# Sparse attention on one core: a new start, scores by halves, half masks near the end, and moved transposes

## Chip, cores, metric

The kernel runs on one core of one Trainium2 chip. The metric is the device time of the whole kernel in microseconds (us), as the median of several executions. A profile's span is about 1.8 us shorter than the time of the same execution (233.0 us against 234.81 us in the kernel before). Engines in the profile: PE is the matmul engine, PEld its weight loads, DVE the vector engine, ACT the scalar engine, POOL the GpSimd engine, SP the engine that issues the loads.

## The reference

Attention over 4 x 8 = 32 heads, 512 queries, 1024 keys, head size 64, with a random mask in which about 10% of the entries are 1. All inputs are fp32. The mask alone is 64 MiB of the 88.08 MB that are read.

```python
def reference(q, k, v, sparse_mask):
    scale = 1.0 / np.sqrt(q.shape[-1])
    scores = scale * np.matmul(q, k.transpose(0, 1, 3, 2))
    scores = np.where(sparse_mask > 0, scores, -1e9)
    attn = np.exp(scores - np.max(scores, axis=-1, keepdims=True))
    attn = attn / (np.sum(attn, axis=-1, keepdims=True) + 1e-8)
    return np.matmul(attn, v).astype(np.float32)
```

## The kernel before

Scores are made with keys on the partitions. A matmul of a mask block against 30 times the identity adds 30 to the entries that stay, and the exp takes 30 away again, so the mask costs matmuls and nothing else. A head has four steps (g = 0 to 3). In each, PE makes scores and adds the mask, ACT takes the exp of 128x1024 elements, and PE multiplies with v one step later.

```python
def scores(h, g):                      # heads 0 to 29
    stg = p_st.tile([128, 2, SQ], FP32, name="stg")
    for i in range(2):                 # two key tiles, all 512 queries
        c = 2 * g + i
        nc.tensor.matmul(stg[:, i, :], kt(h, c), qt(h, c, 0, NQ), start=True, stop=False)
    for i in range(2):
        for t in range(NQ):            # needs all four query blocks of the mask
            nc.tensor.matmul(stg[:, i, ts(t, 128)], mask_weights(h, t, 2 * g + i), cid[:],
                             start=False, stop=(t == NQ - 1))
    pt = expo(stg, [128, 2, SQ])
    return lambda: values(h, g, pt)
# ... heads 30 and 31 go by quarters of the queries, with their masks loaded in quarters ...

with tc.manual_schedule(engines=ordered):      # every engine runs in program order
    for n in range(3):
        load(n)                                # n = 0: mask, then q, k, then v
    # ... constants ...
    convert_qk(0)
    for step in range(4):
        transposes(0, step)                    # q and k of four heads, turned by PE, copied by DVE
    convert_v(0)
    steps = {(1, 2): 0, (2, 0): 1, (2, 2): 2, (3, 1): 3}
    pending = lambda: None
    for h in range(NHEADS):
        if h + 3 < NHEADS:
            load(h + 3)                        # every fourth also loads q, k of the next four heads
        for g in range(NG):
            if g == 1 and h + 1 < NHEADS:
                convert_v(h + 1)
            if (h % GH, g) == (1, 1) and following:
                convert_qk(following)
            todo = quarter_scores(h, g) if quarters else scores(h, g)
            if (h % GH, g) in steps and following:
                transposes(following, steps[h % GH, g])
            pending()
            pending = todo
```

The softmax here doesn't subtract the row's maximum and nothing guards it: scores larger than these inputs give would overflow.

## Time and profile before

| | |
|---|---|
| time | 234.78 us median of 4 (234.44 to 235.03) |
| span of the profile | 233.0 us |
| PE busy | 190.3 us (82%) |
| DMA engines | busy from the second of 40 slices to the 38th |
| mean rate | 398 GB/s over the span, 400 to 436 GB/s in nearly all full slices |

These are lines of the page of the kernel before: span, busy time of PE, the busy tenths of PE, PE's granted clock, busy tenths and rate of the DMA engines in 40 slices, the DMA queue of kind "instruction", and the shares of the chain that ended last.

```profile
span 233.0 us, 5967 instructions
...
PE 190.3 (82%) x2608; PEld 144.1 (62%) x2608; DVE 129.7 (56%) x228; ACT 143.8 (62%) x129; POOL 18.3 (8%) x39
...
PE   0022589899989998999899859996799959999993
...
PEclk9999999999999999999999988999799997999999
DMA  7999999999999999999999999999999999999931
GB/s 239 416 432 425 425 419 422 415 429 425 425 422 400 436 414 427 419 417 435 407 431 417 420 431 418 424 405 436 423 421 419 410 429 427 416 421 403 368 115 23
...
q8 instruction: 20, 0.33, 0.6%
...
DMA 41%; PE 30%; DVE 16%; ACT 8%; issue 3%; SPq 1%; ACTq 0%
...
```

DMA is at 9 (90% or more) nearly throughout, PE is not: the input stream sets the pace.

The next lines are from the timeline of the start of the kernel before (start, duration, engine, line, operation, and in brackets the idle time before and its releaser).

```profile
...
9.85 1.29 DVE L101 TENSOR_SCALAR q<-qf 128x1024 f16<-128x1024 f32 x2 [9.85 <-DMA qf<-in_q_dram]
...
13.50 2.41 DVE L127 COPY qT<-tp 128x512 f16<-128x512 f16 x2
...
15.97 1.04 PE L123 MATMUL tp<-id,q 128*128 128x128 f16 x8 [3.74 <-DVE qT L127]
...
26.61 0.61 PE L157 MATMUL stg<-qT,kT 64*128 64x512 f16 x2 [2.52 <-DVE kT L127]
...
```

PE's first transposes have to wait for a vector copy of 2.4 us before the next ones can use the one PSUM buffer, and the first scores come at 26.61 us.

The timeline of the kernel before around the end of head 25 and the start of head 26:

```profile
...
188.01 0.71 PE L162 MATMUL stg<-cid,mask 128*128 128x128 bf16 x8
...
189.63 0.43 DVE L134 CAST v<-vf 128x512 f16<-128x512 f32 x1 [2.41 <-DMA vf<-in_v_dram]
...
191.32 0.62 PE L123 MATMUL tp<-id,q 128*128 128x128 f16 x8 [2.60 <-DVE q L101]
...
193.80 0.61 PE L157 MATMUL stg<-qT,kT 64*128 64x512 f16 x2
...
194.85 1.07 PE L162 MATMUL stg<-cid,mask 128*128 128x128 bf16 x8 [0.44 <-DMA mask<-in_sparse_mask_dram]
...
```

PE stops at 188.7 us, in the middle of head 25, because the transposes wait for a conversion of q (2.60 us of idle), which the vector engine does only after a conversion of v that itself waits for a load. Then the scores of one step of head 25 (192.12 us) and the values of its last steps are still to do. The first mask matmul of head 26 is at 194.85 us, released by the mask load. Its eight matmuls take 1.07 us, where the usual figure is 0.72.

The timeline of the kernel before at the first mask weights of head 29:

```profile
...
213.04 0.60 PEld L162 LDWEIGHTS <-mask 128*128 128x128 bf16 x8 [0.41 <-DMA mask<-in_sparse_mask_dram]
...
```

The load released them after 0.41 us. The timeline of the kernel before at the end, from the mask matmuls of the last quarter:

```profile
...
227.66 0.72 PE L213 MATMUL stg<-cid,mask 128*128 128x128 bf16 x8
...
229.64 0.43 PE L227 MATMUL av<-v,pt 128*128 128x65 f16 x8 [0.81 <-ACT pt L150]
...
230.32 0.28 DVE L237 TENSOR_SCALAR o<-av,rz 128x64 f32<-128x64 f32 x1
```

Head 29 is the last whose mask PE waited for. From there PE runs without a wait of more than 0.3 us, except for the last exp (0.81 us).

### The profile page before, as it was taken

To read this page: it belongs to the slowest core of one execution; us is meant where nothing else is said; L and a number is where in the kernel's file an instruction comes from. 1 tells how busy PE (TensorE), PEld (TensorE's weight loads), DVE (VectorE), ACT (ScalarE), POOL (GpSimd) and SP (SyncE) were. 2 spreads that over 40 slices of the span, in tenths; PEclk is the share of its full clock that TensorE was granted. 3 is DMA by queue.
4 is the path that set the end of the run, shared out by engine and by line. 5 is a ranking of instruction groups with operands and counts; after the bars stand their busy time and mean duration, and the time that the engine had idled before them with its cause. 6 is when DMAs were issued, how large, how long until landed. Compare 5 with 4: busy or idle time off the path is not lost.

```text
span 233.0 us, 5967 instructions
## 1 busy us (share of the span) xinstructions
PE 190.3 (82%) x2608; PEld 144.1 (62%) x2608; DVE 129.7 (56%) x228; ACT 143.8 (62%) x129; POOL 18.3 (8%) x39
## 2 busy tenths in 40 slices
PE   0022589899989998999899859996799959999993
PEld 0011367677777677777677637774677747766782
DVE  0267506883688358845884177822796156851232
ACT  0000167768866886788677816687277854778873
POOL 2000001010101010101010000100000000101000
PEclk9999999999999999999999988999799997999999
DMA  7999999999999999999999999999999999999931
GB/s 239 416 432 425 425 419 422 415 429 425 425 422 400 436 414 427 419 417 435 407 431 417 420 431 418 424 405 436 423 421 419 410 429 427 416 421 403 368 115 23
DMA packets 14890, 92.66 MB, mean 398 GB/s; under 512 B 2768, under 2 KB 2768, under 8 KB 9872
## 3 DMA queue, kind: packets, MB, share of 16 engines
q1 hardware_dynamic: 13424, 88.35, 91.5%
q0 software_dynamic: 1440, 3.93, 4.3%
q8 instruction: 20, 0.33, 0.6%
q14 instruction: 6, 0.05, 0.1%
HBM read 88.08 MB, written 4.19 MB: 396 GB/s over the span
## 4 chain that ended last, share of the span: by engine, by line
DMA 41%; PE 30%; DVE 16%; ACT 8%; issue 3%; SPq 1%; ACTq 0%
DMA mask<-in_sparse_mask_dram 36%; PE stg L162 10%; DVE qT L127 9%; ACT pt L150 7%; PE av L179 6%; PE stg L157 5%; DMA kf<-in_k_dram 4%; PE tp L123 4%; DVE k L107 2%; PE stg L213 2%; DVE kT L127 2%; DVE q L101 1%; PE stg L204 1%; PE av L227 1%; DVE oo L193 1%
## 5 line engine op out<-in xcount | busy, mean ns | idle before, releaser
L150 ACT ACTIVATE pt<-stg,biasC 128x1024 f16<-128x1024 f32 x128 | 142.5, 1114 | 57.5 <-PE stg L162 50.6
L162 PEld LDWEIGHTS <-mask 128*128 128x128 bf16 x960 | 72.8, 152 | 30.7 <-issue 26.6
L162 PE MATMUL stg<-cid,mask 128*128 128x128 bf16 x960 | 90.0, 240 | 1.5 <-DMA mask<-in_sparse_mask_dram 1.4
L179 PE MATMUL av<-v,pt 128*128 128x65 f16 x960 | 50.8, 197 | 2.8 <-ACT pt L150 1.0
L157 PE MATMUL stg<-qT,kT 64*128 64x512 f16 x240 | 48.5, 400 | 2.5 <-DVE kT L127 2.5
L179 PEld LDWEIGHTS <-pt 128*128 128x128 f16 x960 | 40.0, 100 | 8.0 <-ACT pt L150 8.0
L127 DVE COPY qT<-tp 128x512 f16<-128x512 f16 x32 | 39.8, 1344 | 9.1 <-PE tp L123 9.1
L127 DVE COPY kT<-tp 128x512 f16<-128x512 f16 x32 | 39.9, 1346 | 5.1 <-PE tp L123 5.1
L191 DVE RECIPROCAL rz<-av 128x4 f32<-128x4 f32 x30 | 5.6, 186 | 59.2 <-PE av L179 59.2
L199 POOL DMA_DIRECT2D out_dram<-oo x30 | 17.1, 570 | 201.9 <-DVE oo L193 201.9
L123 PE MATMUL tp<-id,q 128*128 128x128 f16 x128 | 11.1, 236 | 25.9 <-DVE q L101 20.1
L123 PEld LDWEIGHTS <-q 128*128 128x128 f16 x128 | 8.5, 107 | 27.2 <-DVE q L101 20.7
L150 ACT ACT_TABLE_LOAD x1 | 1.3, 1283 | 28.3 <-PE stg L162 28.3
L134 DVE CAST v<-vf 128x512 f16<-128x512 f32 x32 | 13.4, 421 | 8.8 <-DMA vf<-in_v_dram 8.8
L157 PEld LDWEIGHTS <-kT 64*128 64x128 f16 x240 | 11.5, 93 | 9.5 <-DVE kT L127 2.8
L101 DVE TENSOR_SCALAR q<-qf 128x1024 f16<-128x1024 f32 x16 | 10.3, 685 | 9.8 <-DMA qf<-in_q_dram 9.8
L123 PE MATMUL tp<-id,k 128*128 128x128 f16 x128 | 10.7, 231 | 6.1 <-DVE kT L127 2.5
L193 DVE TENSOR_TENSOR oo<-av,rz 128x256 f32<-128x256 f32 x30 | 12.7, 424 | 1.2
L123 PEld LDWEIGHTS <-k 128*128 128x128 f16 x128 | 8.2, 103 | 7.6 <-DVE kT L127 2.8
L107 DVE CAST k<-kf 128x2048 f16<-128x2048 f32 x8 | 9.7, 1215 | 1.2 <-DMA kf<-in_k_dram 1.2
L213 PE MATMUL stg<-cid,mask 128*128 128x128 bf16 x64 | 5.7, 233 | 0.0
L213 PEld LDWEIGHTS <-mask 128*128 128x128 bf16 x64 | 4.7, 150 | 0.8
(16 smaller groups left out, 18.1 us busy)
## 6 DMA issues: line engine op xcount, KB each, us to landing
mask<-in_sparse_mask_dram SPq DMA_DIRECT2D x29, 2048.0 KB, 27.1
kf<-in_k_dram SPq DMA_DIRECT2D x8, 1024.0 KB, 27.2
vf<-in_v_dram SPq DMA_DIRECT2D x16, 512.0 KB, 25.9
qf<-in_q_dram SPq DMA_DIRECT2D x8, 512.0 KB, 26.3
mask<-in_sparse_mask_dram SPq DMA_DIRECT2D x8, 512.0 KB, 20.2
out_dram<-oo POOLq DMA_DIRECT2D x30, 128.0 KB, 6.5
mask<-in_sparse_mask_dram SPq DMA_DIRECT2D x2, 1024.0 KB, 6.3
out_dram<-o SPq DMA_DIRECT2D x8, 32.0 KB, 1.8
```

The lines of the kernel that those rows point to most:

```text
L101: nc.vector.tensor_scalar_mul(out=q16[:, :, x, :], in0=g["qf"][:].rearrange("p (r d) -> p r d", r=RQ), scalar1=scale,)
L107: nc.vector.tensor_copy(out=k16[:].rearrange("p r d -> p (r d)"), in_=g["kf"][:])
L123: nc.tensor.transpose(tp[:, a, e, :], src, ident16[:])
L127: nc.vector.tensor_copy(out=dst[:, :, :, j::GH].rearrange("m x e p -> m e x p"), in_=tp[:, a, :, :].rearrange("m e (x p) -> m e x p", x=GH),)
L134: nc.vector.tensor_copy(out=v16[:, :, 0:D], in_=S[h]["vf"].rearrange("p (t d) -> p t d", t=NK))
L150: nc.scalar.activation(out=pt[:], in_=stg[:], func=EXP, bias=biasC[:], scale=1.0)
L157: nc.tensor.matmul(stg[:, i, :], kt(h, c), qt(h, c, 0, NQ), start=True, stop=False)
L162: nc.tensor.matmul(stg[:, i, ts(t, 128)], mask_weights(h, t, 2 * g + i), cid[:], start=False, stop=(t == NQ - 1),)
L179: nc.tensor.matmul(st["av"][:, t, :], pt[:, i, ts(t, 128)], st["v16"][:, c, :], start=(c == 0 and t == 0), stop=(c == NK - 1), skip_group_ ...
L193: nc.vector.tensor_tensor(out=oo[:], in0=av[:, :, 0:D], in1=rz[:].broadcast_to([128, NQ, D]), op=MULT,)
L199: nc.gpsimd.dma_start(os_[:, h, :], oo[:].rearrange("p t d -> p (t d)"))
L213: nc.tensor.matmul(stg[:, c % 2, c // 2, :], mask_weights(h, t, c), cid[:], start=False, stop=True, skip_group_check=True,)
```

## The change

The intent: q and k first and two engines for the first copies, so that PE starts earlier; scores by half of the queries and half of the keys, so that a head can begin with half its mask; masks 26 to 29 in halves for that; transposes and the conversion of v one step later; and a last exp in two pieces.

```diff
+    STEPS = [(1, 3), (2, 1), (2, 3), (3, 1)]
@@ transposes(i, step)
-        tp = p_tp.tile([128, 2, 4, 128], FP16, name="tp")
+        if i == 0 and step % 2 == 1:
+            tp = p_st.tile([128, 2, 4, 128], FP16, name="stg")
+        else:
+            tp = p_tp.tile([128, 2, 4, 128], FP16, name="tp")
 ...
-            nc.vector.tensor_copy(
+            copy = nc.scalar.copy if i == 0 and step % 2 == 1 else nc.vector.tensor_copy
+            copy(
@@ scores and values: half of the queries (y), half of the keys (g)
-    def scores(h, g):
-        stg = p_st.tile([128, 2, SQ], FP32, name="stg")
-        for i in range(2):
-            c = 2 * g + i
+    def scores(h, y, g):
+        stg = p_st.tile([128, 2, 2, 256], FP32, name="stg")
+        for i in range(4):
+            c = 4 * g + i
             nc.tensor.matmul(
-                stg[:, i, :], kt(h, c), qt(h, c, 0, NQ), start=True, stop=False
-            )
-        for i in range(2):
-            for t in range(NQ):
+                stg[:, i % 2, i // 2, :],
+                kt(h, c),
+                qt(h, c, 2 * y, 2),
+                start=(i < 2),
+                stop=False,
+                skip_group_check=True,
+            )
+        for i in range(4):
+            for t in range(2):
                 nc.tensor.matmul(
-                    stg[:, i, ts(t, 128)],
-                    mask_weights(h, t, 2 * g + i),
+                    stg[:, i % 2, i // 2, ts(t, 128)],
+                    mask_weights(h, 2 * y + t, 4 * g + i),
                     cid[:],
 ...  (values: the same loops; the first and last matmul of a group are marked to match)
@@ quarter_scores(h, t): only the last quarter of the last head
+        if h == NHEADS - 1 and t == NQ - 1:
+            sides = [
+                p_st.tile([128, NG, 128], FP32, name="stg"),
+                p_tp.tile([128, NG, 128], FP32, name="tp"),
+            ]
 ...
+        for x in range(2):
+            for c in range(x, NK, 2):
+                nc.tensor.matmul(sides[x][:, c // 2, :], mask_weights(h, t, c), cid[:], ...)
+            if h == NHEADS - 1 and t == NQ - 1:
+                exp(pt[:, x, :, :], sides[x][:])
 ...  (head 30: the four quarters are stored by one DMA instead of four)
@@ load(n)
         if n == 0:
-            load_mask(0, parts=2)
             load_qk(0)
-            load_v(0)
-            return
         if n % GH == 2 and n // GH + 1 < NHEADS // GH:
             load_qk(n // GH + 1)
-        if n % 2 == 0:
+        if n % 2 == 0 and n:
             load_v(n // 2)
-        load_mask(n, parts=mask_parts(n))
+        load_mask(n, parts=NQ if n >= NHEADS - 2 else (1 if 0 < n < 26 else 2))
+        if n == 0:
+            load_v(0)
@@ the main loop
-        steps = {(1, 2): 0, (2, 0): 1, (2, 2): 2, (3, 1): 3}
 ...
-                if g == 1 and h + 1 < NHEADS:
+                if g == 2 and h + 1 < NHEADS:
                     convert_v(h + 1)
-                if (h % GH, g) == (1, 1) and following:
-                    convert_qk(following)
-                todo = quarter_scores(h, g) if quarters else scores(h, g)
-                if (h % GH, g) in steps and following:
-                    transposes(following, steps[h % GH, g])
+                if g == 1 and x == 1 and more:
+                    convert_qk(i)
+                todo = quarter_scores(h, g) if quarters else scores(h, g // 2, g % 2)
+                if (x, g) in STEPS and more:
+                    transposes(i, STEPS.index((x, g)))
```

## The prediction

> **What bounds the kernel now.** The input stream. The page's slices show the DMA engines at 9 from the second slice to the 38th, nearly all of them at 400 to 436 GB/s; 92.66 MB at 422 GB/s are 220 us of the 233.0 us span. (The Trainium skill, "DMA: Bandwidth & Descriptors", section "Bandwidth", measured 425 GB/s for 16 MB; this trace agrees.) PE is 82% busy and starts late: the timeline shows q converted at 9.85 us, transposes and copies in turn (2.4 us of DVE copies per 1.03 us of transposes), first scores at 26.6 us. But PE has caught up by 133 us: the timeline shows it idle around 135, 163 and 190 us, released by loads of q, k, v, then by masks. The chain of waits has three mask loads of 27 to 29 us, the last ending at 213.0 us.
>
> From there PE is the limit. Head 29's mask lands whole at 213.0 us (PE waited 0.4 us). The last three heads take 5.35 us each (steps of 1.22 to 1.44 us), so the last mask matmuls end at 228.4. The trace's completion records put the last quarter of mask 31 near 225.5 us, so PE is some 2.2 us behind the stream. Then come exp 1.17, values 0.43, DVE 0.5 and the last store, to 233.0.
>
> **What the change does.**
> 1. q and k ahead of mask 0, half the first copies on ACT with a second PSUM buffer: first scores near 15 us (estimate: q lands 4 us earlier, two copy pairs of 2.4 us leave DVE). Worth almost nothing at the end: the bytes are the same and the stream was full; PE just waits more afterwards.
> 2. Scores by half of the queries and half of the keys: same columns, 240 more matmuls and weight loads. The quarter heads, with still smaller pieces, already run at 1.23 and 1.45 us a step, so no cost. The 128x1024 exp stays at 1.11 us.
> 3. Masks 26 to 29 land in halves, and PE can start on the first: 1 MB at 420 GB/s is 2.5 us earlier at head 26. Transposes after (1,3) no longer hold back scores behind q, k, v. Against it: PE idles before head 26, and after such gaps eight mask matmuls take 1.07 instead of 0.72 us (half clock, as in the Trainium skill, "TensorE: Matmul & The Clock Gate", Part 1; the windows' granted clock of 0.91 to 0.96 there agrees). Replayed with before's landing times, head 29 begins 1.8 us earlier.
> 4. The last quarter's exp in halves: 0.5 us less tail.
> 5. Head 30 stored in one DMA: off the critical path.
>
> **Sum.** 1.8 + 0.5 = 2.3 us off the critical path. Both limits then meet: PE's last step and the last mask quarter near 225.5 us, after which some 5 us are needed. Predicted: 232.4 us, 8 in 10 between 230.4 and 234.2. Chances: faster by over 2% (under 230.1) 0.11, within 2% 0.88, slower 0.01.
>
> **What would show it.** First scores near 15 us; DMA slices still full; more PE idle time before masks in the first half; a wait for the mask at the last quarters; mean step still 1.33 us; last input landing within 1 us of 225.5; two last exps of about 0.65 us.
>
> **What would make it wrong.** The last landing moving: its completions spread over 6 us, so a better balance of the DMA engines could give 2 to 3 us more, and more instruction fetches take 1. A colder PE in the last heads would eat the gain.

## The result, and the profile after

The changed kernel took 232.63 us (median of 11, 232.25 to 233.56), the kernel before 234.79 us in the same rounds. The ratio is 0.9915, with a 95% interval of 0.9900 to 0.9929. It is faster by 0.9%, within the 2% band, and 0.2 us from the predicted 232.4.

The same lines of the page, of the changed kernel:

```profile
span 230.5 us, 6446 instructions
...
PE 192.6 (84%) x2848; PEld 150.0 (65%) x2848; DVE 124.9 (54%) x224; ACT 148.8 (65%) x134; POOL 21.3 (9%) x40
...
PE   0559689996999839999499977999499996999994
...
PEclk9999958999999976999979997999979999999999
DMA  7999999999999999999999999999999999999961
GB/s 263 413 430 429 423 417 431 410 426 429 418 426 400 419 435 421 424 409 432 420 428 409 421 431 419 429 412 425 416 429 424 400 418 417 420 414 409 411 252 26
...
q8 instruction: 22, 0.36, 0.6%
...
DMA 83%; PE 10%; DVE 2%; ACT 2%; issue 1%; ACTq 0%; SPq 0%
...
```

The stream is as full as before; the chain is now 83% DMA. Queue 8 has 22 pieces instead of 20.

The timeline of the changed kernel at the start:

```profile
...
4.22 1.30 DVE L99 TENSOR_SCALAR q<-qf 128x1024 f16<-128x1024 f32 x2 [4.22 <-DMA qf<-in_q_dram]
...
14.70 0.61 PE L157 MATMUL stg<-qT,kT 64*128 64x256 f16 x4 [2.52 <-ACT kT L129]
...
```

The first scores come at 14.70 us, 12 us earlier. At the end 2.5 us of span are gained, so nearly all of this is lost on the way: PE just waits for masks.

The timeline of the changed kernel around head 26:

```profile
...
190.28 0.61 PE L124 MATMUL tp<-id,q 128*128 128x128 f16 x8
...
191.07 0.39 PE L157 MATMUL stg<-qT,kT 64*128 64x256 f16 x4
...
193.40 0.72 PE L167 MATMUL stg<-cid,mask 128*128 128x128 bf16 x8 [1.94 <-DMA mask<-in_sparse_mask_dram]
...
```

Head 25 is finished without a stop, and PE waits 1.94 us for the first half of mask 26, at 193.40 instead of 194.85 us. These mask matmuls run at full clock (0.72 us).

The timeline of the changed kernel at the end, from the first mask matmuls of the last quarter:

```profile
...
225.35 0.47 PE L228 MATMUL stg<-cid,mask 128*128 128x128 bf16 x4
...
226.51 0.69 ACT L151 ACTIVATE pt<-tp,biasC 128x512 f16<-128x512 f32 x1
...
227.26 0.30 PE L248 MATMUL av<-v,pt 128*128 128x65 f16 x4 [0.28 <-ACT pt L151]
...
```

The trace's completion records have the last mask quarter in at 225.16 us, and PE uses it from 225.35 us on. So both limits do meet here, to within 0.2 us. The last exp is now one of 0.69 us.

Two pieces of the chain in order of time, of the changed kernel (start, duration, what):

```profile
...
167.36 25.99 DMA mask<-in_sparse_mask_dram
...
193.40 0.72 PE stg L167 x8
...
```

From 193.40 us on the chain has no load any more. What is gained at head 26 is gained at the end. First mask matmuls, from the timelines: head 26 at 194.85 before and 193.40 after (1.45 us), head 30 at 218.39 and 216.12 (2.27 us). Of the 0.82 us between them, 0.46 us come between heads 26 and 27, where the kernel before runs at half clock until 196.07 us, and the rest where it waits for masks 28 and 29. From the first mask matmul of head 31 to the end of the span, it is 9.3 us before and 9.1 us after, so the split exp gives about 0.2 us.

### The profile page after: what moved, and what is told of

The parts are those of the page before. It is cut to its first block, busy times and chain, and to the rows that moved or that the text cites. A ratio compares the mean times of both kernels' runs of the same rounds, so it can differ in the third digit from the quotient of the medians.

```text
span 230.5 us, 6446 instructions
## 1 busy us (share of the span) xinstructions
PE 192.6 (84%) x2848; PEld 150.0 (65%) x2848; DVE 124.9 (54%) x224; ACT 148.8 (65%) x134; POOL 21.3 (9%) x40
## 4 chain that ended last, share of the span: by engine, by line
DMA 83%; PE 10%; DVE 2%; ACT 2%; issue 1%; ACTq 0%; SPq 0%
DMA mask<-in_sparse_mask_dram 81%; PE stg L167 3%; DMA kf<-in_k_dram 2%; PE stg L228 2%; ACT pt L151 2%; PE av L185 2%; PE stg L157 1%; DVE qT L129 1%; PE stg L218 1%; PE av L248 1%; PE tp L124 1%; DVE kT L129 1%; ACTq L350 0%; SPq L72 0%; DVE o L264 0%
## 5 line engine op out<-in xcount | busy, mean ns | idle before, releaser
L185 PE MATMUL av<-v,pt 128*128 128x65 f16 x960 | 52.5, 199 | 1.3
L157 PE MATMUL stg<-qT,kT 64*128 64x256 f16 x480 | 49.2, 285 | 2.5 <-ACT kT L129 2.5
L185 PEld LDWEIGHTS <-pt 128*128 128x128 f16 x960 | 41.9, 102 | 5.4 <-ACT pt L151 5.3
L129 DVE COPY qT<-tp 128x512 f16<-128x512 f16 x30 | 36.8, 1328 | 12.9 <-PE tp L124 12.9
L129 DVE COPY kT<-tp 128x512 f16<-128x512 f16 x30 | 37.7, 1355 | 8.6 <-PE tp L124 8.6
L205 POOL DMA_DIRECT2D out_dram<-oo x30 | 19.6, 653 | 197.2 <-DVE oo L199 197.2
L157 PEld LDWEIGHTS <-kT 64*128 64x128 f16 x480 | 13.8, 95 | 9.6 <-ACT kT L129 2.8
L124 PEld LDWEIGHTS <-q 128*128 128x128 f16 x128 | 10.6, 121 | 5.6 <-DVE q L99 5.6
L124 PE MATMUL tp<-id,k 128*128 128x128 f16 x120 | 9.7, 226 | 4.3 <-DVE qT L129 3.0
L129 ACT COPY qT<-stg 128x512 f16<-128x512 f16 x2 | 2.4, 1344 | 5.5 <-PE stg L124 5.5
```

Of the source, the lines that this page charges most:

```text
L124: nc.tensor.transpose(tp[:, a, e, :], src, ident16[:])
L129: copy(out=dst[:, :, :, j::GH].rearrange("m x e p -> m e x p"), in_=tp[:, a, :, :].rearrange("m e (x p) -> m e x p", x=GH),)
L157: nc.tensor.matmul(stg[:, i % 2, i // 2, :], kt(h, c), qt(h, c, 2 * y, 2), start=(i < 2), stop=False, skip_group_check=True,)
L185: nc.tensor.matmul(st["av"][:, 2 * y + t, :], pt[:, i % 2, i // 2, ts(t, 128)], st["v16"][:, 4 * g + i, :], start=(y == 0 and g == 0 and i ...
L205: nc.gpsimd.dma_start(os_[:, h, :], oo[:].rearrange("p t d -> p (t d)"))
```

## A look at the DMA completions

Each load is spread over the DMA engines and reports 16 completions. A tile is ready with the last of them. The trace has the times of all. The spread from first to last of one load is 0.5 us at 23 us in the changed kernel and 5.2 us at the end. It does not grow evenly. In these two kernels it steps up by 1.0 to 1.6 us from one load to the next at three places, and these places follow the fetches of PE's own instructions, which queue 8 brings in pieces of 16 KB:

```
kernel        pieces  first, 9th, 17th piece at us    spread of the loads (us) around the 17th
before          20     36.9  113.3  200.9             3.83 (landing 201.0) -> 5.33 (207.5)
changed         22     22.9  102.6  183.5             3.81 (landing 183.9) -> 5.08 (186.4)
```

The Trainium skill, "Runtime: NRT & Kernel Launch", section "Instruction fetch mechanics", says that instructions are refilled in blocks of 16 KiB, 256 instructions, by DMA, and that the cost is mostly hidden. The trace agrees on size and count: in the kernel before the pieces come at PE instruction 234, 500, 775, 1041 and so on, 255 apart on average. On the cost it differs. The list of waits shows no wait of PE for its instructions, but a piece takes about 1.07 us (its duration in the packet records), and after every eighth piece the last completion is later for good.

The 16 completions of single loads of the changed kernel show how. Just after the 17th piece (183.5 us), one completion is late: of the load that is complete at 186.40 us, 15 come within 3.86 us of the first, the last 5.09 us after it. After the 18th piece (191.5 us) two are late (load complete at 195.86 us: 5.10 and 5.17 us). After the first piece it was one (29.55 us: 2.13 us, the others within 0.51 us), after the second two (35.84 us). Before the 17th piece, half of them lie in a late group (178.71 us: eight within 1.34 us of the first, eight at 2.97 to 3.39 us). So each piece makes one more completion late, and the ninth and the 17th begin a new round. My reading is that the pieces go round eight DMA engines. The records do not name the engine, so the round is inferred from these counts.

This matters because the 17th piece comes when PE has run 4354 to 4378 matmuls and weight loads, in all runs that reach it but one (4363 in the kernel before; 4290 in a_avt24 below). A kernel with more PE instructions reaches it earlier, and from then on every load is complete some 1.2 to 1.6 us later than without it. The second step follows its piece too: in a_avt below the ninth piece comes at 138.2 us in place of 102.6, and the spread rises from 1.98 us (landing 138.2) to 3.34 us (144.7).

## The experiments

Each ran against the kernel before on the same chip and in the same rounds of timing; all gave correct results. "Changed" in a diff's heading means that the edit is made to the changed kernel, "before" that it is made to the kernel before. Landing times are from the completion records; the head times are first mask matmuls in the timelines. One profile is one execution, and the median is of several.

| run | 17th piece | mask 26: first half / whole | head 26 | head 27 | last quarter | time us | ratio |
|---|---|---|---|---|---|---|---|
| before | 200.9 | - / 194.80 | 194.85 | 201.44 | 225.53 | 234.79 | 1 |
| changed | 183.5 | 193.35 / 195.86 | 193.40 | 199.53 | 225.16 | 232.63 | 0.9915 |
| after_again | 183.4 | 192.95 / 195.59 | 192.99 | 200.20 | 224.87 | 232.37 | 0.9899 |
| a_whole | 183.6 | - / 195.95 | 196.00 | 204.11 | 224.65 | 236.09 | 1.0061 |
| a_one_exp | 183.3 | 193.56 / 196.08 | 193.61 | 199.73 | 225.31 | 232.68 | 0.9920 |
| a_old_start | 183.4 | 193.59 / 196.04 | 193.64 | 200.91 | 225.20 | 234.04 | 0.9969 |
| a_old_steps | 182.6 | 193.38 / 195.87 | 196.27 | 203.01 | 225.21 | 235.37 | 1.0023 |
| b_start | 200.7 | - / 194.63 | 194.86 | 200.98 | 224.97 | 234.64 | 0.9995 |
| b_layout | 182.5 | - / 196.37 | 196.42 | 202.86 | 225.02 | 236.18 | 1.0052 |
| b_half | 183.4 | 194.01 / 196.43 | 196.40 | 202.53 | 225.53 | 235.85 | 1.0053 |
| a_wide | 196.0 | 191.64 / 194.43 | 191.69 | 198.36 | 225.05 | 232.15 | 0.9891 |
| w_old_start | 196.4 | 191.90 / 194.68 | 192.05 | 198.74 | 225.41 | 232.62 | 0.9904 |
| a_avt | none | 191.74 / 194.23 | 193.06 | 199.37 | 223.70 | 231.41 | 0.9846 |
| a_avt24 | 224.9 | 191.85 / 194.62 | 192.20 | 198.67 | 223.82 | 232.42 | 0.9900 |

The theory at first: the stream sets the pace, and the end is set by when PE can begin head 26 and how fast it goes from there. Rivals: the early start is the gain; or the moved transposes are; or the halves alone. Later a second theory came in: instruction fetches delay the loads.

### after_again: the changed kernel once more

No edit.

> The changed kernel once more, as the yardstick of this series: 232.2 to 233.6 us, 0.989 to 0.994 of the kernel before. Its runs fell into two groups, near 232.4 and near 233.5; if the cause is where instruction fetches fall among the DMA engines, a profile of the slower group shows the first half of mask 26 landing about 1 us later; if it is the PE clock, it shows half clock in head 26.

Measured: 232.37 us (232.08 to 232.93). The profile fell on the slowest execution, 232.93 us, though the first half of mask 26 landed 0.4 us earlier (192.95 us) than in the first profile. Stretch 195 to 198 us of the view by windows, here of the first profile of the changed kernel (the line of columns says what they are: busy times with instruction counts, granted PE clock, DMA share, rate):

```profile
...
core 0: us, PE busy (x) PEld busy (x) DVE busy (x) ACT busy (x) POOL busy (x), PEclk, DMA share, GB/s
...
195.00:198.00 3.00, 3.00 (x54) 2.47 (x52) 2.23 (x3) 2.34 (x3) 0.54 (x1) 1.00 1.03 421
...
```

The same stretch of this run:

```profile
...
195.00:198.00 3.00, 3.00 (x35) 2.50 (x34) 1.93 (x2) 1.11 (x1) 0.49 (x1) 0.52 1.02 415
...
```

PE did 54 matmuls in this stretch at clock 1.00, and 35 at 0.52. Heads 26 to 27 take 6.13 us in one profile and 7.21 us in the other: 1.08 us, about the distance of the two groups of runs (232.25 to 232.70 and 233.36 to 233.56 us in the first series). The Trainium skill, "TensorE: Matmul & The Clock Gate", section "What's actually happening", says that the clock is halved after an idle window of about 3.4 us, and that this window runs freely. The traces agree on the window: in the clock records of all profiles the stretches begin and end on a grid of 3.413 us, and those at half clock within the kernel are one or two windows long. They show that the window need not be idle throughout: an idle gap of 1.53 us halved the clock here, while one of 1.94 us left it alone in the first profile. The grid tells the two apart. In the first profile an edge at 192.76 us cuts the gap into 1.30 and 0.64 us; here the gap lies within one window (191.07 to 194.49 us). The position is not the whole rule: in other windows, of five of the profiles, gaps of 1.64 to 1.76 us did not halve the clock. That the slower group of runs is the one at half clock is likely, but not shown: the profile at half clock (232.93 us) lies between the groups, with a mask that landed 0.4 us earlier.

### a_whole: the changed kernel, masks 26 to 29 whole

```diff
-        load_mask(n, parts=NQ if n >= NHEADS - 2 else (1 if 0 < n < 26 else 2))
+        load_mask(n, parts=NQ if n >= NHEADS - 2 else (1 if 0 < n < 30 else 2))
```

> The changed kernel with masks 26 to 29 loaded whole again. Theory (PE is the limit from the first half of mask 26 on): head 26 waits for the whole 2 MB, its first mask matmul is 1.4 to 2.5 us later, PE may cool in the longer gap, and 1.4 to 2.3 us come back: 233.9 to 234.8 us. Rival (the gain came from the early start or from the transposes' new places): under 0.3 us come back.

Measured: 236.09 us, ratio 1.0061. More than the whole gain comes back: 3.7 us against after_again. The timeline at head 26:

```profile
...
196.00 1.08 PE L167 MATMUL stg<-cid,mask 128*128 128x128 bf16 x8 [4.14 <-DMA mask<-in_sparse_mask_dram]
...
```

Head 26 begins at 196.00 us, 2.6 us later than in the changed kernel, and takes 8.11 us to head 27 instead of 6.13, at half clock for 6.8 us in the records. The theory's direction holds, its size was too small. And a surprise: the other parts of the change without the halves make a kernel that is slower than before. Its mask 26 is complete at 195.95 us, that of before at 194.80. This led to the look at the completions above.

### a_one_exp: the changed kernel, last exp undivided

```diff
-        if h == NHEADS - 1 and t == NQ - 1:
-            sides = [ ...two tiles... ]
+        if False: ...
-            if h == NHEADS - 1 and t == NQ - 1: exp(pt[:, x, :, :], sides[x][:])
+        exp(pt[:], stg[:])
```

> The changed kernel with the last quarter's exp undivided. Theory: the tail after the last mask matmul gets 0.3 to 0.6 us longer: 232.7 to 233.1 us. Rival (the two instructions cost what they save): no difference above 0.1 us.

Measured: 232.68 us against 232.37; the intervals of the ratios (0.9899 to 0.9941 and 0.9886 to 0.9912) overlap, so the times do not settle it. In the profiles, head 31 to the end takes 9.3 us here, 9.1 us in the two of the changed kernel. So it is worth about 0.2 us, less than the 0.5 predicted.

### a_old_start: the changed kernel with the old start

```diff
         if n == 0:
+            load_mask(0, parts=2)
             load_qk(0)
+            load_v(0)
+            return
-        if i == 0 and step % 2 == 1: tp = p_st.tile(...)
+        tp = p_tp.tile([128, 2, 4, 128], FP16, name="tp")
-            copy = nc.scalar.copy if i == 0 and step % 2 == 1 else nc.vector.tensor_copy
+            copy = nc.vector.tensor_copy
```

> The changed kernel with the start of before: mask 0 ahead of q and k, all first copies on the vector engine, one PSUM buffer. Theory (the stream sets the pace, PE catches up by a third of the span): first scores near 26 us again instead of 14.7, and the end moves by less than 0.4 us. Rival (the early start gives the gain): 234.5 us or more.

Measured: 234.04 us (233.73 to 234.49), ratio 0.9969. This missed what the theory expected (under 0.4 us): it costs 1.7 us against after_again. In the profile the half mask lands at 193.59 us, 0.24 us after that of the first profile of the changed kernel, and heads 26 to 27 take 7.27 us, at a granted clock of 0.55 between 195 and 198 us. Both together are 1.4 us, which is the whole distance of the two profiled executions (233.76 and 232.37 us). It does not explain why all five runs were slow, so the start was tried in two more places. As it stands, the changed kernel without the new start keeps 0.7 of its 2.4 us.

### b_start: the kernel before with the new start alone

```diff
-            load_mask(0, parts=2)
             load_qk(0)
+            load_mask(0, parts=2)
             load_v(0)
```
(and the copies on ACT and the second PSUM buffer, as in the change)

> The kernel before with the new start alone (q and k first, half the first copies on the scalar engine, a second PSUM buffer). Theory (the stream sets the pace): first scores at 14.7 instead of 26.6 us and at the end within 0.5 us of before, 234.3 to 234.9, at most the 0.2 to 0.3 us by which the loads get going faster (0.42 against 0.29 MB moved by 3 us). Rival (the start gives the gain, as putting the old start back into the changed kernel cost 1.4 to 1.7 us): 233.0 to 233.6 us.

Measured: 234.64 us against 234.74, ratio 0.9995 (0.9981 to 1.0009). The first mask matmul of the kernel is at 15.31 us, and head 26 begins at 194.86 us, as before. The new start alone is worth nothing. As the sole cause, that rival falls.

### b_layout: the kernel before with scores by halves

```diff
-    def scores(h, g): ...two key tiles, 512 queries...
+    def scores(h, y, g): ...four key tiles, 256 queries, as in the change...
-                todo = quarter_scores(h, g) if quarters else scores(h, g)
+                todo = quarter_scores(h, g) if quarters else scores(h, g // 2, g % 2)
```

> The kernel before with the scores by half of the queries and half of the keys, masks whole as before. Theory A (my prediction): same columns, no cost, 234.5 to 235.0. Theory B (from the traces): PE's instructions come by DMA in pieces of 16 KB, every eighth of them on the same DMA engine, which then lags the others by 1.5 us more; 480 more instructions bring the 17th piece from 200.9 us to about 187 us, so mask 26 lands at 195.6 to 196.0 instead of 194.8 and the kernel takes 235.3 to 236.3 us.

Measured: 236.18 us (235.10 to 236.41), ratio 1.0052: slower by 1.4 us, as theory B had it, and not "no cost" as my prediction had it. The line of instruction pieces in the DMA view of this run (pieces, MB, share):

```profile
...
q8 instruction: 22, 0.36, 0.6%
...
```

Its first mask matmuls of head 26 in the timeline:

```profile
...
196.42 1.05 PE L167 MATMUL stg<-cid,mask 128*128 128x128 bf16 x8 [0.18 <-DMA mask<-in_sparse_mask_dram]
...
```

The 17th piece comes at 182.5 instead of 200.9 us. Mask 26 is complete at 196.37 instead of 194.80 us. The load was not issued later (167.78 and 167.66 us), and 14 of its 16 completions are in by 194.66 us, as before (194.64); only the last two are late, 195.72 and 196.37 us against 194.75 and 194.80. PE's own pace is not touched: heads 29 to 30 take 5.35 us in both. No run changes the number of instructions alone; here the order of the scores changes with it.

### b_half: the same, with masks 26 to 29 in halves

```diff
-        return 4 if h >= NHEADS - BY_QUARTERS else 1
+        return 4 if h >= NHEADS - BY_QUARTERS else (2 if h >= 26 else 1)
```

> The same, and masks 26 to 29 in halves. Theory (half masks are the gain, later landings are a cost): first half of mask 26 at about 193.4, head 26 begins 1.4 us before that of before, 2 to 3 us less than the run with the new order of scores and whole masks: 233.0 to 234.0 us. Rival (halves only help with the new start or the new places of the transposes): within 0.5 us of that run.

Measured: 235.85 us, ratio 1.0053, within 0.5 us of b_layout. The rival is right. The first half lands at 194.01 us, but PE only gets to head 26 at 196.40 us, because it was held in head 25 from 189.2 to 192.67 us by the transposes. The halves need the other places of the transposes.

### a_old_steps: the changed kernel, old places of transposes and v

```diff
-    STEPS = [(1, 3), (2, 1), (2, 3), (3, 1)]
+    STEPS = [(1, 2), (2, 0), (2, 2), (3, 1)]
-                if g == 2 and h + 1 < NHEADS:
+                if g == 1 and h + 1 < NHEADS:
                     convert_v(h + 1)
```

> The changed kernel with the transposes and the conversions of v at their old places. Theory (halves pay only when PE isn't held in head 25 by the loads of q, k and v): PE is blocked from 188.5 to about 192.5 us with two steps of head 25 still to do, head 26 begins near 196 us although its first half lands near 193.5, and nearly the whole gain goes: 235.0 to 236.0 us. Rival (the places don't matter): 232.2 to 233.6 us.

Measured: 235.37 us, ratio 1.0023. The whole gain goes, and 0.5 us more. The timeline of this run:

```profile
...
190.64 0.43 DVE L136 CAST v<-vf 128x512 f16<-128x512 f32 x1 [3.73 <-DMA vf<-in_v_dram]
...
192.33 1.03 PE L124 MATMUL tp<-id,q 128*128 128x128 f16 x8 [3.69 <-DVE q L99]
...
196.27 1.07 PE L167 MATMUL stg<-cid,mask 128*128 128x128 bf16 x8
...
```

The first half of mask 26 was in at 193.38 us, the whole at 195.87. PE came at 196.27 us: the vector engine waited 3.73 us for v and turned to q only then. Half masks and moved transposes are worth something only together.

### a_wide: full-width scores where masks are whole

A version built on the finding: heads 1 to 25 go back to the old scores, which removes 400 PE instructions.

```diff
-                todo = quarter_scores(h, g) if quarters else scores(h, g // 2, g % 2)
+                todo = (quarter_scores(h, g) if quarters
+                        else wide_scores(h, g) if 0 < h < 26 else scores(h, g // 2, g % 2))
```
(wide_scores and its values are the loops of the kernel before)

> The changed kernel with the scores of heads 1 to 25 at full width again, whose masks are whole anyway: 400 PE instructions fewer. Theory B: the 17th instruction piece comes after 194 us, the first half of mask 26 lands near 192 instead of 193.3 us, PE hardly idles before head 26 and doesn't drop to half clock there, and the runs' upper group near 233.5 goes; the last mask quarter still lands near 225 us and is then what PE waits for: 231.8 to 232.4 us. Rival (fetches don't matter): as the changed kernel, two groups.

Measured: 232.15 us (232.11 to 232.49), ratio 0.9891. The timeline at the first mask matmuls of heads 26, 27 and 28:

```profile
...
190.88 0.39 PE L195 MATMUL stg<-qT,kT 64*128 64x256 f16 x4
...
191.69 0.73 PE L205 MATMUL stg<-cid,mask 128*128 128x128 bf16 x8 [0.41 <-DMA mask<-in_sparse_mask_dram]
...
198.36 0.72 PE L205 MATMUL stg<-cid,mask 128*128 128x128 bf16 x8 [0.47 <-DMA mask<-in_sparse_mask_dram]
...
205.20 0.72 PE L205 MATMUL stg<-cid,mask 128*128 128x128 bf16 x8 [1.20 <-DMA mask<-in_sparse_mask_dram]
...
```

The 17th piece comes at 196.0 us, after the first half of mask 26 has landed (191.64 us, 1.7 us earlier than in the changed kernel). PE waits 0.41 us instead of 1.94 and stays at full clock. None of the four runs is near 233.5. All of this is as theory B said. What it had wrong is the last wait: that is not for the last quarter (in at 225.05 us, used from 225.19 us) but for the first half of mask 28, which lands at 205.16 us, 0.17 us later than in the changed kernel. So PE waits 1.20 us there, head 31 begins at 221.28 instead of 221.45 us, and little more is gained at the end.

### w_old_start: a_wide with the old start

> The kernel with full-width scores in heads 1 to 25 (232.15 us) with the old start. Theory (the old start in the changed kernel cost 1.4 to 1.7 us only through later landings near head 26 and half clock there, not by the start itself): here PE hardly idles before head 26, so at most 0.5 us come back: 232.1 to 232.7 us. Rival (the start is worth 1.4 us when halves are in): 233.5 us or more.

The edit is that of a_old_start. Measured: 232.62 us (232.52 to 232.65), 0.5 us slower than a_wide. So the start is worth 0.5 us at most here. The half masks land 0.26 us later at head 26 (191.90 against 191.64 us) and 0.15 us later at head 28 (205.31 against 205.16 us), whose mask PE waits for in both. The rest of what a_old_start lost is gone once PE hardly idles before head 26. This fits the half clock as the cause there, without showing it. Why all five runs of a_old_start were slow is left open.

### a_avt: fewer than 4362 PE instructions

Built on a_wide: in heads 1 to 25, v becomes the weights and the probabilities the 512 moving columns. The 65x512 result is copied to fp16 and turned back by four transposes.

```diff
-            for t in range(NQ):
-                nc.tensor.matmul(st["av"][:, t, :], pt[:, i, ts(t, 128)], st["v16"][:, c, :], ...)
+            nc.tensor.matmul(st["avT"][:], st["v16"][:, c, :], pt[:, i, :], ...)
+        # after the last step: copy to oT, then, one step later
+        for t in range(NQ):
+            nc.tensor.transpose(av[:, t, 0 : D + 1], oT[:, ts(t, 128)], ident16[0 : D + 1, 0 : D + 1])
```

> As the kernel with full-width scores in heads 1 to 25, but these heads multiply with v as the weights and the probabilities as 512 moving columns, and turn the 65x512 result back by four transposes: 1000 PE instructions fewer. In the traces piece number 17 of PE's instructions is fetched at instruction 4362 to 4374; this kernel has 4298, so it never comes. Theory B: no DMA engine gets a third lag of 1.5 us, the last mask quarter lands at 223.4 to 224.0 instead of 225.1 and the kernel takes 230.4 to 231.4 us, if PE keeps up with the stream in heads 1 to 25 (estimate 6.1 us a head with transposes of q and k, against 6.5 us a head of the stream). Rival (the lag has another cause): last landing 225 us, 232 us or more.

Measured: 231.41 us median of 6 (five of 231.00 to 232.28 and one of 234.03), ratio 0.9846 (0.9833 to 0.9859; the plain mean of all six runs gives 0.9873). The line of instruction pieces in the DMA view of this run:

```profile
...
q8 instruction: 16, 0.26, 0.5%
...
```

Its first mask matmuls of head 26 in the timeline, without a wait for the mask:

```profile
...
193.06 0.72 PE L215 MATMUL stg<-cid,mask 128*128 128x128 bf16 x8
...
```

There are 16 pieces. The spread of the loads stays at 3.9 us, and the last mask quarter is in at 223.70 us, 1.35 us earlier than in a_wide. This is what theory B expected and its rival did not. Head 26 begins at 193.06 us although half its mask was there at 191.74: PE, with heads 24 and 25 at 5.8 and 6.2 us, is now the limit. So the earlier loads did not shorten the profiled execution: its head 31 begins at 221.32 us, against 221.28 in a_wide. Why four of the others are about 1 us faster is not shown. The execution of 234.03 us was not the profiled one (232.28 us) and stays unexplained. The kernel is correct and the fastest of all by its median.

### a_avt24: v as weights in heads 0 to 23 only

```diff
+        if h >= 24:
+            ...multiply with v as the kernel before does...
-                        else wide_scores(h, g) if 0 < h < 26 else scores(h, g // 2, g % 2))
+                        else wide_scores(h, g) if h < 26 else scores(h, g // 2, g % 2))
```

> As the kernel with v as the weights, but only in heads 0 to 23; heads 24 and 25 multiply with v as before, and head 0 too has full-width scores: 4322 PE instructions, still under 4362. In the run before, the stream was through at 223.7 us but PE was the limit, with heads 24 and 25 at 6.2 and 5.8 us and the first mask matmul of head 26 at 193.06. Theory: still 16 instruction pieces and a last landing near 223.7 us; head 26 begins about 0.7 us earlier; 230.4 to 231.0 us, best of all. Rival (a 17th piece comes after all, or something else limits): 231.4 us or more.

Measured: 232.42 us (231.44 to 232.59), ratio 0.9900: worse than a_avt, against the expectation. Its profiled execution was its fastest, at 231.44 us: head 26 begins at 192.20 us, 0.9 us earlier, and the last quarter lands at 223.82 us, both as expected. A 17th piece did come, at 224.9 us (after 4290 matmuls and weight loads, earlier than in all other runs), after the last load. The four slower executions have no profile, so their cause stays open. The profiled one has no half clock between 171 and 228 us; whether the others had one is not shown (their mean granted clock is 0.970, against 0.975).

## Why the prediction was right or wrong

- **The total was right.** Predicted 232.4 us with 230.4 to 234.2; measured 232.63. The direction was right, and so was the path: head 26 begins on half its mask, and PE is the limit from there on, as the chain of the changed kernel shows. That the size fits so well is partly luck. The sum was 1.8 us (head 29 begins earlier) and 0.5 us (last exp); the first profile has 2.27 us (213.04 and 210.77 us) and 0.2 us, so two errors cancel.
- **"Worth almost nothing at the end" (the start): right for the kernel before, open for the changed one.** First scores at 14.70 us, near the predicted 15; alone it gives a ratio of 0.9995, in w_old_start its absence costs 0.5 us. But a_old_start lost 1.7 us in the changed kernel itself. Of this, 1.4 us are seen in one profile as later landing and half clock; why it struck all five runs stays open.
- **"Same columns, 240 more matmuls and weight loads ... so no cost": wrong.** It costs 1.4 us alone (b_layout against before). I looked for the cost on PE, where there is none. It is in the stream: the 17th instruction piece comes 18 us earlier, and mask 26 is complete 1.57 us later.
- **"1 MB at 420 GB/s is 2.5 us earlier at head 26": too large.** The term measured 1.45 us (194.80 to 193.35). A half does land 2.5 us before the whole in the same run (193.35 and 195.86), but the whole had moved 1.06 us later.
- **The half clock after the gap: half right.** I counted it in every run. It was absent in the first profile (0.72 us for eight mask matmuls, clock 1.00) and present in the second (0.52), where head 29 begins 1.60 us earlier (211.44 us). Its absence made up for the term above.
- **"Transposes after (1,3) no longer hold back scores": right, and bigger than I had it.** Without it the halves are worth nothing (a_old_steps 235.37, b_half 235.85 us).
- **The last exp: 0.2 us in place of 0.5.** "Two last exps of about 0.65 us": 0.69 us for the one shown.
- **"A wait for the mask at the last quarters": not seen.** The two limits met so closely (225.16 and 225.35 us) that none was left. "Last input landing within 1 us of 225.5" is right.
- **Head 30 in one DMA** was not tried by itself.
- **"More instruction fetches take 1"** stood among the things that could make it wrong. It did happen, and should have stood in the sum.

## What to carry to other kernels

Where DMA is the limit and PE runs behind it, trace the end back to the last load that PE waited for: only what makes that load land earlier, or lets PE start on part of it, comes out at the end, and an obstacle elsewhere in PE's order can undo it (here the half masks without the moved transposes). Splitting matmuls into smaller ones with the same columns is not free even when PE shows no longer step: instructions are loaded too, and here each piece of them made a part of the data's loads land later. Look at the spread of a load's completions, not only at the mean rate, and count instructions before splitting everywhere what only a few heads need.

## What the Trainium skill lacked or had wrong

- "Runtime: NRT & Kernel Launch", section "Instruction fetch mechanics", gives 16 KiB blocks of 256 instructions and calls their cost mostly hidden. The runs agree on the blocks (20 pieces for 5216 PE matmuls and weight loads). They show a cost in a kernel limited by DMA: each 16 KB piece takes about 1.07 us and makes one more of a load's 16 completions late, and with the first, ninth and 17th piece the last completion moves by 1.0 to 1.6 us in the kernels before and after. Smaller matmuls with 480 more instructions cost 1.4 us of 235, and staying under the 17th piece moved the last landing from 225.05 to 223.70 us.
- "DMA: Bandwidth & Descriptors", section "Bandwidth", has the rate, but no figure for the spread of completions within one load: 0.5 to 1.0 us at the start and 5 to 6 us at the end of the kernels after and before, at 400 to 436 GB/s in nearly all full slices.
- "TensorE: Matmul & The Clock Gate" speaks of an idle window of about 3.4 us. A gap well under that was enough: 1.53 us before head 26, all within one window of the 3.413 us grid, was followed by half clock (0.52 between 195 and 198 us); 1.94 us in another run of the same kernel, cut by an edge of the grid, was not. It made 1.08 us between heads 26 and 27.
